# One step of a hybrid diffusion backbone on one core: running sums started in PSUM by ScalarE, units turned, products and head squares moved to ScalarE

## The chip, the core and the metric

The kernel runs on one core of one Trainium2 chip. The metric is the device time of one execution in microseconds (us), as the median of several runs. Five engines work side by side, each through its own list of instructions in order: PE (TensorE, the matrix multiplier), DVE (VectorE), ACT (ScalarE), POOL (GpSimd) and SP (SyncE, which here only issues DMAs). PE writes its sums to PSUM, which this kernel uses as 8 banks of 128x512 fp32; everything else lies in SBUF.

## The reference

Two groups of 128 tokens (a context group, `s=0`, and a latent group, `s=1`), width 2048, go through one layer.

```python
sh1, sc1, g1, sh2, sc2, g2 = split(silu(c) @ w_ada + b_ada, 6)
h = rms_norm(x, norm1_w) * (1 + sc1) + sh1                 # 128 x 2048 each group
qa, ka, va, qb, kb, vb, ga, gb = split(h @ w_in)           # 2048 -> 8704 columns
oa, ob = attention(qa, ka, va), attention(qb, kb, vb)      # QK-norm, rotary, softmax
merged = sigmoid(ga) * (oa @ w_br_a) + sigmoid(gb) * (ob @ w_br_b)
x = x + g1 * (merged @ w_out)
h2 = rms_norm(x, norm2_w) * (1 + sc2) + sh2
x = x + g2 * (relu(h2 @ w_up) ** 2 @ w_down)               # 2048 -> 8192 -> 2048
```

All inputs and outputs are fp32.

## The kernel before

**A step.** The weights are read once, in tiles of 128x1024 (512 KB: two blocks of 128 rows by 512 columns). A step of the kernel is the work on one such tile; there are 456, in an order fixed when the kernel is built. To reach fp32 accuracy each tile is split: ACT copies it to the type fp32r (`wH`, L93), DVE takes the difference tile minus copy (`wL`, L241), and PE forms three products for each pair of operands: high by high, high by low, low by high (L291 to L293 in a `unit`, L391 to L393 in the first stage). An ordinary step has 12 matmuls of 128x512 (2 row blocks x 2 token groups x 3 products). The two token groups have a PSUM bank each.

**What sets the order.** Every engine's list is written out by hand in `run` (L264): for each step it first issues the DMA loads that the table `RUN` makes due, then splits tiles up to `LOOK` steps ahead, then writes the step's matmuls and, at a unit's end, its evacuation, and last what is hung on that step with `at`. So an instruction of ACT or DVE waits behind all that was written before it, above all behind the splits of later tiles. The pool `pacc` has 4 banks, given out in turn; the pool `paux` has the other 4.

**First stage, the K passes.** The projection `h @ w_in` for nine column blocks (units qA 0 and 1, kvA, qB 0 and 1, kB 0 and 1, vB 0 and 1) goes over the 16 row blocks of K in five passes (`CHUNKS`: 2, 2, 2, 4, 6 row blocks), because `h` becomes known bit by bit: PE, in `pair_mm`, computes the modulation (sc1, sh1) from `w_pair` between the steps. In each pass every unit starts two fresh banks; at its end the sum is copied to SBUF by ACT in the first pass (`first_evac`, L372), and added to the SBUF sum by DVE in the later four (L400). A unit of the passes of 2 row blocks is one step. Passes 1 and 2 are steps 9 to 17 and 18 to 26.

**Middle.** The eight gate units, and between their steps the attention: `qk_stat` (L618) squares the heads on ACT and sums the squares on DVE (L624); `normalise` (L740) multiplies the softmax numerators by 1/denominator on DVE (L746). Then the branch products, `w_out`, the second norm (`norm2`, L970) and the first two units of `w_up`.

**Last stage, up pairs and down pieces.** The 8192 columns of `w_up` are done as 8 pieces of two blocks. Seven of them are "pairs" (`up_pair`, L1107) in which some row blocks, listed in `FAST`, use Strassen's scheme: 7 products in place of 8. For such a fast position DVE forms sums of weight blocks (`prep_y`, L1164: `t` L1172, then L1175 to L1177, then the low parts `XL`, `tL`, `uL`, L1180 to L1182) and ACT the high parts (`XH`, `YB`, `tH`, `uH`). A pair uses all 8 banks: Q1, Q6, Q2, Q7 of `pacc`, Q3, Q4, Q5, Z of `paux`. After each pair come four down units (`down_unit`, L1246), one for each block of 512 output columns, over that piece's 1024 rows of `w_down`: 4 steps each. A down unit's two banks are copied to `dsum` by ACT for piece 0, added to `dsum` by DVE (L1257), or, where listed in `SUM_DMA`, copied by ACT and added by a DMA that POOL issues. `gate_sum` (L1234) multiplies `dsum` by g2 and adds it to x at piece 6; the last piece multiplies its own banks by g2 and adds (`resid`, L902).

**The places that matter below.** A pair begins while the last down unit's banks are being emptied: its second product takes the bank of that unit's first group, its third the bank of the second group. A pair ends with five products (Q2, Q7, Q4, Q5, Q3) after Q6; the down unit behind it takes the banks of Q1 (first group) and Q6 (second group). `silu_cond` (L1307) computes SiLU of the condition row each time it is loaded (`load_cond`, L1302), five times two rows in all.

Of the kernel before, what the change touches and what calls it, by code (L numbers as in the profile page):

```python
# [18 lines left out]
P = 128  # L19
# [15 lines left out]
H_AT = 41  # L35
DOTS1 = [11, 17, 20, 28, 28, 31, 34, 37]
# [5 lines left out]
GATE_BACK = 8  # L42
DIRECT = (3,)
LO_DMA = [70, 83, 107, 131, 176, 184, 233, 292, 314, 328, 402, 404]
LO_AHEAD = 2

LOOK = "443323444122344433223333332123333453344534333554455544344534333543324554444555556665556644444333333333332222122312344544555434333333342344333334333323445566643344456656533344434444445455564546555553444554322355444554433333333434334533333333333654544332334455543444555653215536544523333334543233333332223323365455455443222212233432443334434642333334444544534434333333333325434222223333434444444434555642255353443444442222432331122132223342112223332233345544"
RUN = "301110000000010212223333322222222221111122244455544355434445554334554445555664543433234334444445665543321222222212444444444444442222222232223344444455544544444444555455454445566644455555554543365434343355445756644443566664333312222234552332223333334545332333333333322211122222332233322212233323323332332112344444442343322211333343334323233334544422742222212223445554422333233322222211222333333435767545333110221112232111233456655566567556433435335553333334"
CONST_AT = [65, 67]
XL_DMA = []  # L50
ADA_AT = [None, 4, 13, 18, 21, 36, 29]
XS_AT = {1: 13, 2: 18, 3: 29}
POST = {('kvA', 0): [67, 70, 75], ('qA', 0): [70, 73, 78], ('qA', 1): [72, 74, 80], ('kB', 0): [77, 83, 90], ('qB', 0): [82, 84, 93], ('kB', 1): [86, 91, 93], ('qB', 1): [90, 93, 97]}
JOBS = [[79, 80, 80, 87, 93], [81, 83, 88, 90, 93], [87, 87, 89, 90, 99], [93, 93, 96, 99, 102], [96, 97, 100, 105, 112], [102, 103, 107, 112, 123], [105, 107, 111, 118, 123], [112, 115, 118, 121, 123]]
SS_AT = [43, 51, 73, 75, 139, 139]
T_AT = [4, 4]
PREP_IN = [6, 7]
DOTS = [33, 39, 42, 43, 47, 47, 48, 49, 52, 54, 55, 57, 60, 62, 69, 70, 73, 77, 80, 84, 90, 91, 92, 92, 94, 98, 101, 103, 103, 105, 108, 110, 111, 112, 115, 118, 120, 121, 122, 122, 126, 127, 128, 129, 130, 132, 132, 136, 137, 138, 138, 143, 144, 147, 147, 150, 153, 155, 157, 161, 164, 167, 170, 172, 173, 174, 175, 176, 177, 178, 179, 182]
DOTS2 = [230, 232, 234, 235, 236, 237, 240, 243, 255, 263, 265, 269, 270, 288, 301, 301, 307, 328, 328, 331, 333, 334, 358, 360, 361, 363, 366, 368, 391, 391, 395, 399]
STAT_AT = [-1, 0, 10, 16]  # L60
T_PAIR = [[8, 9], [6, 8], [8, 9], [7, 8], [10, 11], [8, 9], [12, 11]]
P_PAIR = [[4, 2], [2, 4], [3, 4], [1, 3], [6, 6], [3, 3], [6, 5]]
M_TE = (3,)
M_AT = [1, 3, 9]
FLIP = 1
P_UP = [4, 1]
# [5 lines left out]
def tile_hybrid_step(ctx: ExitStack, tc: tile.TileContext, a):  # L72
# [210 lines left out]
    def mm3(acc, stat, st, first, last, order=(0, 1)):  # L283

        wh, wl = st["hl"]
        for k in range(2):
            kk = 2 * st["half"] + k
            for tb in order:
                sh, sl = stat(kk, tb)
                f, l = first and k == 0, last and k == 1  # L290
                pe.matmul(acc[tb], sh, wh[:, k, :], start=f, stop=False)  # L291
                pe.matmul(acc[tb], sh, wl[:, k, :], start=False, stop=False)  # L292
                pe.matmul(acc[tb], sl, wh[:, k, :], start=False, stop=l)  # L293
# [77 lines left out]

    def first_evac(u, acc):  # L372
        units[u] = G(f"u_{u[0]}{u[1]}").rearrange("p (s n) -> p s n", s=2)
        for tb in range(2):
            copy(units[u][:, tb, :], acc[tb])

    def start_steps(u, k0, nk):

        box = {}

        def mm(st, kt):
            if kt == 0:
                box["acc"] = [bank("acc", pacc) for _ in range(2)]
            acc = box["acc"]
            wh, wl = st["hl"]
            last = kt + 2 == nk
            for k in range(2):
                g, kg = divmod(k0 + kt + k, 4)
                for tb in range(2):
                    sh, sl = hH[g][:, kg, tb, :], hL[g][:, kg, tb, :]  # L390
                    pe.matmul(acc[tb], sh, wh[:, k, :], start=kt == 0 and k == 0, stop=False)  # L391
                    pe.matmul(acc[tb], sh, wl[:, k, :], start=False, stop=False)  # L392
                    pe.matmul(acc[tb], sl, wh[:, k, :], start=False, stop=last and k == 1)  # L393
            if not last:
                return
            if k0 == 0:
                first_evac(u, acc)
                return
            for tb in range(2):
                dve.tensor_tensor(units[u][:, tb, :], units[u][:, tb, :], acc[tb], op=OP.add)  # L400
            box.clear()

        for kt in range(0, nk, 2):
            add_step(wsrc(w_in, k0 + kt, COL[u[0]] + 512 * u[1]), lambda st, kt=kt: mm(st, kt), u)
# [18 lines left out]
    for g, i in XS_AT.items():  # L423
        at(i, lambda g=g: x_scale(g))
    k0 = 0
# [1072 lines left out]
```

## Time and profile before

| | |
|---|---|
| runs, median (lowest to highest) of 3 | 1333.61 us (1331.23 to 1334.71) |
| profiled execution, first to last instruction | 1331.3 us |
| PE busy | 1316.0 us (99%), 6411 instructions recorded |
| DVE busy | 1190.2 us (89%), 1546 |
| ACT busy | 800.8 us (60%), 979 |
| POOL busy | 54.6 us (4%), 64 |
| DMA | 392 MB, mean 295 GB/s |

The profiled execution is one more execution than the three runs; its own time is given as its span, 1331.3 us from the first to the last instruction. That is 2.3 us under the median of the runs and equal to the fastest of them.

In the lists by line, a row gives line, engine, operation, written tile, read tiles, shapes and count, then the busy time in us and the mean of one in ns, then the engine's idle time just before and what ended it. In the windows, each engine has its busy time and, in brackets, its count. In the timeline a row gives start and duration in us; a matmul's duration is 0.39 us because matmuls overlap, so for PE the distance between starts is what counts.

### The profile page before, as it was taken

The numbers are of one execution on the slowest core, as the hardware profiler recorded it, in microseconds if no ns is written. First come the engines' busy times: TensorE is split into PE (matmuls) and PEld (weight loads), VectorE is DVE, ScalarE is ACT, GpSimd is POOL, SyncE is SP. The second block draws the span as 40 slices with busy tenths as digits, with TensorE's granted clock in tenths as the row PEclk, the third lists the DMA queues.
The fourth block names the chain that finished last, engine by engine and source line by source line (L and its number), as shares of the span: only waits on it lengthen the run. The fifth ranks groups of instructions, "written<-read, shape, count | busy, mean of one in ns | idle before, by whom it ended". The sixth has DMA issues, their size and how long they took to land.

```text
span 1331.3 us, 18039 instructions
## 1 busy us (share of the span) xinstructions
PE 1316.0 (99%) x6411; PEld 1067.0 (80%) x6412; DVE 1190.2 (89%) x1546; ACT 800.8 (60%) x979; POOL 54.6 (4%) x64
## 2 busy tenths in 40 slices
PE   8999999999999999999999999999999999999998
PEld 4777778788888878888888888888888888877887
DVE  4699999988898999999779998998999999989685
ACT  5534443476656446635677866758577576676660
POOL 0000000521000000000000000000000000000000
PEclk9999999999999999999999999999999999999999
DMA  9999998986589999996578876988798696878962
GB/s 374 409 409 408 409 401 300 384 277 240 177 329 355 381 392 356 354 367 214 191 230 280 281 254 215 291 273 266 235 296 255 237 301 206 311 195 291 331 213 98
DMA packets 148267, 392.24 MB, mean 295 GB/s; under 512 B 51793, under 2 KB 53009, under 8 KB 148177
## 3 DMA queue, kind: packets, MB, share of 16 engines
q1 hardware_dynamic: 144448, 378.16, 78.8%
q0 software_dynamic: 3584, 12.85, 5.0%
q8 instruction: 50, 0.82, 0.3%
q14 instruction: 41, 0.33, 0.1%
q10 hardware_dynamic: 144, 0.08, 0.0%
HBM read 367.16 MB, written 8.68 MB: 282 GB/s over the span
## 4 chain that ended last, share of the span: by engine, by line
PE 92%; DMA 4%; DVE 2%; ACT 1%; issue 1%; SPq 0%; DVEq 0%; ACTq 0%
PE acc L291 16%; PE acc L292 16%; PE acc L293 16%; PE Q L1117 6%; PE Q L1119 6%; PE Q L1118 6%; PE acc L391 4%; PE acc L392 4%; PE acc L393 4%; DMA araw<-in_w_pair 3%; PE ps_ada L308 2%; PE ps_S L707 1%; PE Z L1119 1%; PE Z L1117 1%; PE Z L1118 1%; DMA aT<-in_w_adaT 1%
## 5 line engine op out<-in xcount | busy, mean ns | idle before, releaser
L241 DVE TENSOR_TENSOR wL<-raw,wH 128x1024 fp32r<-128x1024 f32 x375 | 446.6, 1225 | 72.0 <-ACT wH L93 67.9
L93 ACT ACTIVATE wH<-raw 128x1024 fp32r<-128x1024 f32 (+1 forms) x393 | 392.8, 1044 | 128.3 <-PE acc L392 23.3
L391 PE MATMUL acc<-wH,hH 128*128 128x512 f32 x276 | 109.1, 395 | 0.0
L393 PE MATMUL acc<-wH,hL 128*128 128x512 f32 x276 | 107.5, 390 | 0.0
L392 PE MATMUL acc<-wL,hH 128*128 128x512 f32 x276 | 107.5, 389 | 0.0
L291 PE MATMUL acc<-wH,hH 128*128 128x512 f32 x256 | 101.4, 396 | 0.0
L293 PE MATMUL acc<-wH,hL 128*128 128x512 f32 x256 | 99.7, 390 | 0.0
L292 PE MATMUL acc<-wL,hH 128*128 128x512 f32 x256 | 99.7, 390 | 0.0
L1327 DVE CUSTOM_DVE_ANT_0 aT<-aT,cB,cols 128x1024 f32<-128x1024 f32 x56 | 71.7, 1286 | 0.2
L1327 DVE CUSTOM_DVE_ANT_0 junk<-aT,cB,cols 128x1024 bf16<-128x1024 f32 x56 | 71.4, 1280 | 0.0
L93 ACT ACTIVATE tH<-t 128x1024 fp32r<-128x1024 f32 x33 | 35.0, 1061 | 58.0 <-DVE t L1172 55.4
L391 PEld LDWEIGHTS acc<-wH,hH 128*128 128x128 f32 x276 | 51.8, 188 | 13.6 <-issue 2.5
L393 PEld LDWEIGHTS acc<-wH,hL 128*128 128x128 f32 x276 | 51.8, 188 | 11.0
L392 PEld LDWEIGHTS acc<-wL,hH 128*128 128x128 f32 x276 | 51.8, 188 | 10.4
L293 PEld LDWEIGHTS acc<-wH,hL 128*128 128x128 f32 x256 | 48.0, 188 | 10.2
L291 PEld LDWEIGHTS acc<-wH,hH 128*128 128x128 f32 x256 | 48.1, 188 | 9.8 <-ACT sq L622 0.4
L292 PEld LDWEIGHTS acc<-wL,hH 128*128 128x128 f32 x256 | 48.1, 188 | 9.4
L93 ACT ACTIVATE uH<-raw 128x1024 fp32r<-128x1024 f32 x33 | 35.1, 1063 | 31.6 <-DVE raw L1177 28.6
L1223 ACT ACTIVATE up<-up 128x1024 f32<-128x1024 f32 x28 | 29.7, 1062 | 26.8 <-DVE up L1217 26.3
L308 PE MATMUL ps_ada<-araw,cpad 128*32 128x256 f32 x640 | 39.1, 382 | 2.7 <-DMA araw<-in_w_pair 2.5
L93 ACT ACTIVATE fTa<-pTa 128x2048 uint16<-128x2048 uint16 x16 | 40.5, 2533 | 2.0 <-PE acc L292 1.4
L1172 DVE TENSOR_TENSOR t<-raw 128x1024 f32<-128x1024 f32 x33 | 40.2, 1219 | 1.0 <-PE acc L292 1.0
(641 smaller groups left out, 3316.7 us busy)
## 6 DMA issues: line engine op xcount, KB each, us to landing
raw<-in_w_in SPq DMA_DIRECT2D x133, 512.0 KB, 9.5
raw<-in_w_down SPq DMA_DIRECT2D x128, 512.0 KB, 5.6
araw<-in_w_pair SPq DMA_DIRECT2D x80, 512.0 KB, 10.2
raw<-in_w_upF SPq DMA_DIRECT2D x66, 512.0 KB, 5.2
aT<-in_w_gT SPq DMA_DIRECT2D x64, 512.0 KB, 6.9
raw<-in_w_up SPq DMA_DIRECT2D x62, 512.0 KB, 5.0
aT<-in_w_adaT SPq DMA_DIRECT2D x48, 512.0 KB, 9.6
raw<-in_w_out SPq DMA_DIRECT2D x32, 512.0 KB, 9.6
```

The costliest lines, as they stand in the source:

```text
L93: act.activation(out, in_, AF.Copy)
L241: dve.tensor_tensor(st["lo"], st["raw"], st["hi"].bitcast(F32), op=OP.subtract)
L291: pe.matmul(acc[tb], sh, wh[:, k, :], start=f, stop=False)
L292: pe.matmul(acc[tb], sh, wl[:, k, :], start=False, stop=False)
L293: pe.matmul(acc[tb], sl, wh[:, k, :], start=False, stop=l)
L391: pe.matmul(acc[tb], sh, wh[:, k, :], start=kt == 0 and k == 0, stop=False)
L392: pe.matmul(acc[tb], sh, wl[:, k, :], start=False, stop=False)
L393: pe.matmul(acc[tb], sl, wh[:, k, :], start=False, stop=last and k == 1)
L1117: pe.matmul(acc, stat[0], hi, start=f, stop=False)
L1118: pe.matmul(acc, stat[0], lo, start=False, stop=False)
L1119: pe.matmul(acc, stat[1], hi, start=False, stop=l)
L1327: dve.tensor_tensor_reduce(out, box["raw"], cB[s, tag], 1.0, dst if second else baT[:, part, fb:fb + 1], OP.mult, OP.add, dst)
```

## The change

PE has the same 6020 instructions before and after (counted in the two built programs, with the same operands and shapes). What changes:

- **Down pieces.** A down unit of piece 1 to 7 no longer starts fresh banks. Ahead of it ACT copies the SBUF sum `dsum` into its two banks (`seed`, 56 copies), and its matmuls add on top. At its end ACT copies the banks back to `dsum` (56 copies in place of 28), except in the last piece. The 28 DVE additions, the 10 additions by DMA and `gate_sum` (16 DVE operations) go. The seed is written after the third step before the unit; for the first down unit behind a pair it stands at the end of that pair.
- **K passes.** Of the later passes' units, 22 are seeded in the same way (44 copies in, 44 copies out in place of 44 of the DVE additions). Two more units per pass boundary stay in their banks: passes 1 and 3 run the units in a turned order that begins with vB, so the last two units of one pass are the first two of the next, and 16 further additions go. 12 of 72 remain.
- **Attention.** The product with 1/denominator is 32 ACT instructions of 128 or 256 columns in place of 8 on DVE; the squares are 52 ACT instructions of 128 columns with a running sum in place of 14 wider ones and 7 DVE reductions.
- **Strassen.** In `prep_y` the DVE's order is now t, YB, first sum, XL, second sum, tL, uL. `FAST` keeps its counts (3, 4, 5, 5, 5, 5, 6) and moves positions.
- **Rest.** SiLU of the condition is computed 4 times in place of 10, kept in DRAM and loaded again. `resid` multiplies both groups before it adds. x and g2 are loaded back 8 steps before a unit's end in piece 7, where it was 6 in piece 6. Tables are set anew: `LOOK` at 59 of 456 places and `RUN` at 98, and the places of dot products, attention parts and loads.

ScalarE's list around the start of pair 7, before. `dsum_10517` and `dsum_10694` are the copies that empty the third and fourth down unit's banks; XH, YB, tH, uH are one fast position.

```order
L93 ACTIVATE a13H<-fTa_10566 128x1024
L93 ACTIVATE wH<-raw 128x1024 x2
L93 ACTIVATE XH<-raw 128x1024
L93 ACTIVATE YB<-raw 128x512
L93 ACTIVATE tH<-t_10614 128x1024
L93 ACTIVATE uH<-raw 128x1024
L93 ACTIVATE XH<-raw 128x1024
L93 ACTIVATE YB<-raw 128x512
L93 ACTIVATE tH<-t_10659 128x1024
L93 ACTIVATE uH<-raw 128x1024
L93 ACTIVATE dsum_10694<-acc 128x512 x2
L93 ACTIVATE XH<-raw 128x1024
```

The same place of ScalarE's list in the changed kernel, from the third unit's seed on (`dsum_7148` is the sum of the third unit, `dsum_7219` of the fourth).

```order
L97 ACTIVATE XH<-raw 128x1024
L97 ACTIVATE dsum_7148<-acc 128x512 x2
L97 ACTIVATE YB<-raw 128x512
L97 ACTIVATE tH<-t_10699 128x1024
L97 ACTIVATE uH<-raw 128x1024
L97 ACTIVATE wH<-raw 128x1024 x2
L97 ACTIVATE dsum_7219<-acc 128x512 x2
L97 ACTIVATE XH<-raw 128x1024
L97 ACTIVATE YB<-raw 128x512
L97 ACTIVATE tH<-t_10780 128x1024
L97 ACTIVATE uH<-raw 128x1024
```

The fourth unit's copies moved from behind two fast positions to behind one, with two plain splits between them and it.

ScalarE's list in pass 1 of the changed kernel, from the end of step 10 on (`acc<-u_...` is a seed, `u_...<-acc` the emptying of a unit's banks). Before, this stretch holds splits, modulation work and no copy of a sum.

```order
L97 ACTIVATE u_vB_615<-acc 128x512 x2
L97 ACTIVATE acc<-u_qB_391 128x512 x2
L97 ACTIVATE u_kvA_348<-acc 128x512 x2
L97 ACTIVATE acc<-u_qB_408 128x512 x2
L97 ACTIVATE wH<-raw 128x1024 x2
L97 ACTIVATE u_qB_391<-acc 128x512 x2
L97 ACTIVATE acc<-u_kB_470 128x512 x2
L97 ACTIVATE wH<-raw 128x1024 x2
L97 ACTIVATE u_qB_408<-acc 128x512 x2
L97 ACTIVATE S<-ps_ada 128x512
L97 ACTIVATE acc<-u_kB_511 128x512 x2
```

Each unit's seed stands two units ahead of its matmuls, behind the emptying of the unit whose banks it takes.

ScalarE's list at the end of pair 2 in the changed kernel: `up<-Q` reads bank Q1, and the row behind it seeds the banks of Q1 and Q6 for the first down unit.

```order
L97 ACTIVATE wH<-raw 128x1024 x3
L97 ACTIVATE up_7527<-Q_7231 128x512
L97 ACTIVATE acc<-dsum_6938 128x512 x2
L1267 ACTIVATE up_7527<-up_7527 128x1024 x2
L1267 ACTIVATE up_7528<-up_7528 128x1024 x2
```

The seed was not there before; relu and square (two rows each) now stand behind it.

The core of the diff:

```diff
-FAST = {1: (0, 3, 7), 2: (0, 2, 6, 7), 3: (0, 2, 4, 5, 7), 4: (0, 2, 4, 5, 7), 5: (0, 3, 4, 5, 7), 6: (0, 2, 4, 5, 7), 7: (0, 1, 2, 4, 5, 7)}
-SUM_DMA = [5, 6, 11, 13, 16, 19, 21, 23, 25, 27]
+FAST = {1: (0, 4, 7), 2: (0, 4, 6, 7), 3: (0, 2, 3, 4, 7), 4: (0, 2, 4, 5, 7), 5: (0, 1, 3, 5, 7), 6: (0, 2, 4, 5, 7), 7: (0, 2, 3, 4, 5, 7)}
+SEED_AT = 3
+KEEP = True
+SEED1_AT = 2
+SEED1 = "111111111111111100100001101011111111"
...
+        def seed():
+            seeds1[u] = banks()
+            for tb in range(2):
+                copy(seeds1[u][tb], units[u][:, tb, :])
...
-            if kt == 0:
-                box["acc"] = [bank("acc", pacc) for _ in range(2)]
+            if kt == 0 and u not in held:
+                if seeded and u not in seeds1:
+                    seed()
+                held[u] = seeds1.pop(u) if seeded else banks()
+                opened[u] = not seeded
...
-                    pe.matmul(acc[tb], sh, wh[:, k, :], start=kt == 0 and k == 0, stop=False)
+                    pe.matmul(acc[tb], sh, wh[:, k, :], start=opened[u] and k == 0, stop=False, skip_group_check=skip)
...
+    turned = first_units[7:] + first_units[2:7] + first_units[:2]
...
         for s in range(2):
-            act.activation(sq[:, s].rearrange("p h d -> p (h d)"), raw[:, s, 0:nh * HD], AF.Square)
-        ssq, r = SM(2 * nh, "ssq"), SM(2 * nh, "rq")
-        dve.tensor_reduce(ssq.rearrange("p (s h) -> p s h", s=2), sq, axis=AX.X, op=OP.add)
+            for h in range(nh):
+                act.activation(sq[:, s, h, :], raw[:, s, h * HD:h * HD + HD], AF.Square,
+                               accum_out=ssq[:, s * nh + h:s * nh + h + 1])
...
-            dve.tensor_tensor(prob[:, :, 0:nk], prob[:, :, 0:nk], rd.unsqueeze(2).to_broadcast([P, 4, nk]), op=OP.mult)
+            for h in range(4):
+                act.activation(prob[:, h, 0:nk], prob[:, h, 0:nk], AF.Copy, scale=rd[:, h:h + 1])
...
-                dve.tensor_tensor(Y[:, 0:512], t[:, 0:512], X[:, 512:1024], op=OP.add)
                 dve.tensor_tensor(b["YB"][:, 512:1024], Y[:, 512:1024], b["YB"][:, 0:512].bitcast(F32), op=OP.subtract)
+                dve.tensor_tensor(Y[:, 0:512], t[:, 0:512], X[:, 512:1024], op=OP.add)
+                if 8 * p + pos not in XL_DMA:
+                    dve.tensor_tensor(b["XL"], X, b["XH"].bitcast(F32), op=OP.subtract)
                 dve.tensor_tensor(Y[:, 512:1024], Y[:, 0:512], Y[:, 512:1024], op=OP.add)
                 copy(b["uH"], Y)
...
+                    if p > 1:
+                        seed(p - 1, 0)
...
+    def seed(p, n):
+
+        seeds[p, n] = [bank("acc", pacc) for _ in range(2)]
         for s in range(2):
-            dve.tensor_tensor(d[:, s, :], d[:, s, :], gbc["g2", n][:, s, :], op=OP.mult)
-            dve.tensor_tensor(x1[n][:, s, :], x1[n][:, s, :], d[:, s, :], op=OP.add)
+            copy(seeds[p, n][s], dsum[n][:, s, :])
...
+        if p and (n or p == last):
+            at(len(wsteps) - SEED_AT, lambda: seed(p, n))
```

More of the change, by code (lines that the diff above doesn't have):

```diff
@@ L65 @@
 FLIP = 1
-P_UP = [4, 1]
+P_UP = [2, 1]
 T_UP = [6, 5]
@@ L281, in run, with mm3 @@
                 fn()
-    def mm3(acc, stat, st, first, last, order=(0, 1)):
+    def mm3(acc, stat, st, first, last, seeded=False):
         wh, wl = st["hl"]
@@ L1067, in mm @@
                 if q == 0:
-                    box["acc"] = [bank("acc", pacc) for _ in range(2)]
+                    box["acc"] = seeded()
                 box["hl"][q] = st["hl"]
@@ L1269, in down_unit @@
-        if p == last - 1:
-            at(end_of(("down", p, n)) + 6, lambda: gate_sum(n))
+        unit(a["w_down"], 512 * n, [4 * j for j in PIECES[p]], stat, evac, ("down", p, n), seeded if p else None)
     for n in PIECES[0]:
```

184 lines of the change are left out of this document (106 added, 78 removed).

## The prediction, made before the changed kernel was run

> **What bounds the kernel now.** I read the page first, then the same busy times stage by stage, then the list of what PE waited for, and last the timeline around the one wait that is large.
>
> ```profile
> span 1331.3 us, 18039 instructions
> ## 1 busy us (share of the span) xinstructions
> PE 1316.0 (99%) x6411; PEld 1067.0 (80%) x6412; DVE 1190.2 (89%) x1546; ACT 800.8 (60%) x979; POOL 54.6 (4%) x64
> ```
>
> PE is busy for 99% of the span. The change leaves PE's 6020 instructions as they are, so the 94 us or so that it takes from DVE, and the 131 us that it gives ACT (the counts of the change by the durations below), are worth nothing by themselves. Only what PE waits for can go or come. The stages show where that is (us; busy time and count of PE, weight loads, DVE, ACT, POOL; granted clock, DMA share, GB/s). The rows are the stages of pairs 1, 3, 4 and 7, then passes 1 and 2, then the attention.
>
> ```profile
> 730.46:773.98 43.52, 43.52 (x194) 36.04 (x192) 41.75 (x53) 34.63 (x36) 0.00 (x0) 1.00 0.83 276
> 858.30:898.82 40.52, 40.41 (x178) 33.14 (x177) 40.00 (x45) 22.27 (x25) 0.86 (x1) 1.00 0.85 281
> 942.34:983.16 40.82, 40.42 (x179) 33.15 (x177) 38.84 (x42) 24.70 (x28) 1.73 (x2) 1.00 0.84 288
> 1194.45:1239.26 44.81, 41.21 (x175) 33.67 (x174) 43.75 (x48) 25.03 (x29) 0.87 (x1) 0.96 0.90 309
> 53.10:81.88 28.78, 28.78 (x177) 22.56 (x176) 27.39 (x40) 12.40 (x16) 0.00 (x0) 1.00 1.03 408
> 81.88:114.98 33.10, 33.10 (x246) 24.86 (x244) 30.67 (x51) 14.84 (x19) 0.00 (x0) 1.00 1.03 409
> 233.00:466.00 233.00, 233.00 (x1189) 193.00 (x1188) 210.88 (x298) 136.34 (x243) 33.52 (x31) 1.00 0.84 306
> ```
>
> The first row is PE unhindered: 43.52 us / 192 matmuls = 226.7 ns from one start to the next. At that rate the 177 matmuls of pairs 3 and 4 take 40.13 us, and took 0.39 and 0.69 more. The 174 of pair 7 take 39.45 us, and took 44.81: **5.4 us too many**, with a granted clock of 0.96. PE's own waits, in us in total, times, longest:
>
> ```profile
> PE Q L1117 <- ACT dsum L93: 4.0, 2, 3.6
> PE ps_ada L308 <- DMA araw<-in_w_pair: 2.5, 5, 0.6
> PE acc L461 <- ACT hH L93: 1.3, 2, 0.9
> ```
>
> All else is below 1.3 us. The first row is pair 7's wait. PE's timeline there, the releaser in brackets:
>
> ```profile
> 1195.58 0.39 PE L1119 MATMUL Q<-YB,h20L 128*128 128x512 f32 x1
> 1199.57 0.80 PE L1117 MATMUL Q<-tH,sH 128*128 128x512 f32 x1 [3.60 <-ACT dsum L93]
> 1200.16 0.63 PE L1118 MATMUL Q<-tL,sH 128*128 128x512 f32 x1
> ...
> 1202.72 0.43 PE L1118 MATMUL Q<-tL,sH 128*128 128x512 f32 x1
> ```
>
> Start to start, 1195.58 to 1199.57 is 3.99 us, 3.76 more than 0.227. Then the matmuls start 0.43 us apart until 1202.72: half the rate, another 1.6 us. ACT's rows in that time:
>
> ```profile
> 1197.97 1.06 ACT L93 ACTIVATE uH<-raw 128x1024 fp32r<-128x1024 f32 x1 [1.00 <-DVE raw L1177]
> 1198.94 1.06 ACT L93 ACTIVATE dsum<-acc 128x512 f32<-128x512 f32 x2
> ```
>
> 1195.58 is the pair's sixth matmul, so the down unit's last one started 6 x 0.227 before, at 1194.22, and its banks could have been emptied from about 1194.5. The two copies stand in ACT's list behind the highs of two fast positions, and the last of these, `uH`, waited for DVE. The copies began 4.4 us late.
>
> **The change, part by part.** The sums go against the profiled span, 1331.3 us; the median of the runs is 2.3 us above it, and I add that at the end.
>
> *Pair 7.* In the new list the two copies stand behind one fast position and two plain splits, and that position's ACT work stands behind the third unit's copies, which can run four steps (48 x 0.2267 = 10.9 us) before the pair. So ACT is free in time, and 5.4 us are there to win. What is late next is DVE:
>
> ```profile
> 1201.20 1.22 DVE L1172 TENSOR_TENSOR t<-raw 128x1024 f32<-128x1024 f32 x1
> ...
> 1207.80 2.35 DVE L241 TENSOR_TENSOR wL<-raw,wH 128x1024 fp32r<-128x1024 f32 x2
> ...
> 1231.00 1.22 DVE L1182 TENSOR_TENSOR uL<-raw,uH 128x1024 fp32r<-128x1024 f32 x1
> ```
> ```profile
> 1235.41 0.39 PE L1118 MATMUL Q<-uL,sH 128*128 128x512 f32 x1
> ```
>
> A fast position takes DVE 6.60 us (1201.20 to 1207.80) and PE 21 x 0.2267 = 4.76. A plain one takes DVE about 2.3 and PE 5.44. So DVE loses 1.8 us per fast position and lives on its lead. Before, the last `uL` was ready at 1232.2 and used at 1235.4: 3.2 us of lead, less than the 5.4 that PE is to gain. The new order (0, 2, 3, 4, 5, 7) puts a plain position second. Counted from the pair's start: ACT empties the banks until 1.2, does XH (1.0) and YB (0.6) of position 2 by 2.7; DVE can do `YB` then and, five operations later, has that position's `uL` at about 8.0. Three more fast positions, the plain one and the last (4 x 6.5 + 2.3; 6.5 since the new order no longer makes an operation wait for the one just ahead of it) end at 36.3, or at 35.9 if each takes 6.4. PE wants that `uL` after 34.7 + 4 x 0.2267 = 35.6. I take 0.3 us of wait there (0 to 2.2, the latter if DVE stands to PE as before). Three splits (3.4 us) and the additions stand behind it on DVE, so the seed after the pair is late too, another 0.2. **Pair 7: -4.9 us (-5.4 to -3.2).**
>
> *Pairs 3 and 4.* There, too, ACT now empties the last unit's banks behind a single high part, `XH`. That needs a load to have landed, so I take most of the excess as gone, not all: **-0.3** (-0.4 to 0) and **-0.4** (-0.7 to 0). Pair 5's second position is now fast; by the same count DVE has its `uL` at 7.1 where PE wants it at 8.4.
>
> *Passes 1 and 2.* Durations, as busy us and mean ns:
>
> ```profile
> L93 ACT ACTIVATE dsum<-acc 128x512 f32<-128x512 f32 x28 | 16.0, 594 | 24.3 <-PE acc L293 22.5 <-PE acc L292 1.2
> L93 ACT ACTIVATE wH<-raw 128x512 fp32r<-128x512 f32 x6 | 3.5, 619 | 0.0
> L980 ACT ACTIVATE h2f<-x,r 128x512 f32<-128x512 f32 x4 | 2.7, 713 | 0.5 <-POOL r L136 0.5
> L1257 DVE TENSOR_TENSOR dsum<-dsum,acc 128x512 f32<-128x512 f32 x28 | 18.2, 683 | 2.7 <-PE acc L293 2.7
> ```
>
> Between the ends of steps 9 and 24, 15 ordinary steps with some modulation matmuls between them (53.7 us of PE), ACT gets 28 copies out (0.594) and 24 copies in. A copy from SBUF to PSUM does not occur in the trace. Nearest is the SBUF to SBUF copy of the same shape at 0.619; the ends are 0.594 (the PSUM read) and 0.713. I take 0.619, the row with the same source. That adds 16.6 + 14.9 = 31.5 us to what ACT did there: 12.40 + 14.84 us in 61.9, so 23.6 in 53.7. Together 55 us, less some 3 to 6 since two copies in a row overlap (1.06 us in place of 1.19): 50 us of 53.7. ACT becomes nearly full where it was 44% busy. It keeps up on the whole, and each seed stands two units (5.4 us) ahead. I take **+0.5 us**. The lower end is 0, since PE waits for no bank there now; the upper is 2.9: 0.5 more, and 24 x 0.1 should each seed cost 0.1 more than assumed with nothing to hide it. DVE, 27.39 of 28.78 us busy there, loses 18 units x 2 x 0.683 = 24.6 us, and nothing waited for it.
>
> *Ends of pairs 2 to 7.* The first down unit needs its second bank, Q6's, seeded after DVE's second addition.
>
> ```profile
> 813.46 2.80 DVE L1217 TENSOR_TENSOR up<-up,Q 128x512 f32<-128x512 f32 x4
> ```
> ```profile
> 814.78 0.39 PE L291 MATMUL acc<-wH,a2H 128*128 128x512 f32 x1
> ```
> ```profile
> 1066.78 1.40 DVE L1217 TENSOR_TENSOR up<-up,Q 128x512 f32<-128x512 f32 x2
> ```
> ```profile
> 1067.65 0.40 PE L291 MATMUL acc<-wH,a8H 128*128 128x512 f32 x1
> ```
>
> After pair 2 the addition ends at 814.14 and a copy of 0.62 at 814.8; the bank is wanted three matmuls after 814.78, at 815.46: 0.6 us to spare. After pair 5 the addition ends at 1067.46, the copy at 1068.1, the bank is wanted at 1067.65: **+0.5 us** (0 to 1.0, if one of the others slips). The seeds of the other down units stand three steps (about 8 us) ahead of need.
>
> *Attention.*
>
> ```profile
> L732 ACT ACTIVATE prob<-ps_S,nm 128x128 f32<-128x128 f32 x16 | 5.7, 367 | 10.5 <-DVE nm L730 7.7 <-DVE nm L728 2.7
> ...
> L732 ACT ACTIVATION_READ_ACCUMULATOR prob<-ps_S,nm 128x1 f32 x24 | 4.9, 203 | 0.0
> ...
> L622 ACT ACTIVATE sq<-u_qB 128x512 f32<-128x512 f32 x4 | 2.3, 634 | 0.0
> ```
>
> The squares: 52 x (0.367 + 0.203) less 14 x 0.634 is +20.8 us of ACT. The 32 scalings are 12 to 20 us (0.367 to 0.62 each). In the attention's 233 us ACT would then be busy for some 175 in place of 136.34, and PE never waits there: **0** (0 to 1, where a weight split stands behind such a group). [...]
>
> *The rest.* SiLU, `resid` and the loads change nothing that PE waits for: loads keep their place in SP's list apart from a few steps, and POOL loses ten transfers. The early waits for `araw` and `hH` (3.8 us) keep their causes: **0** (0 to -3.8).
>
> The sum: -4.9 - 0.3 - 0.4 + 0.5 + 0.5 = **-4.6**, a span of 1326.7. With the median's 2.3 us: **1329.0 us**.
>
> **Rivals.** A measurement of this kernel tells 0.3%, 4.0 us, from no change: faster is below 1329.6, slower above 1337.6.
>
> *DVE takes over pair 7, or the wait stays in part.* If DVE stands to PE as it does now, PE gains only DVE's lead: the 5.4 us shrink to 3.2, the sum to -2.9 or, with the other terms at their poor ends, to about 0: 1330.7 to 1334. For it speaks DVE's 43.75 us of work in a stage of 39.45; against it the plain second position and two additions fewer ahead of the pair. On the clock, 1199.57 to 1202.72 shows that the long wait cost 1.6 us beyond itself, and no other row shows how long a wait must be for that. [...]
>
> *Slower: ACT as the gate of all banks.* Every unit now needs ACT twice, and ACT's list is in order. If ACT comes to a down unit's banks as late as it did at pair 7 (5.4 us) at two of the seven pair starts, the sum is -4.6 + 10.8: 1339.8. One such place gives 1334.4, still no change; two decide it. For it: at pairs 3 to 5 the copies stand behind an `XH` that waits for a load. Against it: the same arrangement at pair 4 cost 0.7.
>
> *More than the forecast.* The waits for `araw` and `hH` shrink too, since DVE has room early: up to 3.8 us more, 1325.2.
>
> **How the numbers follow.** The forecast has 0.54 (0.46 of it below 1329.6, 0.08 in the band), the first rival 0.23, all in the band, the slower one 0.13 (0.11 slower, 0.02 in the band), the last 0.10. That makes faster 0.56, same 0.33, slower 0.11. The range: the forecast's own terms give 1326.5 to 1333; it reaches down to 1322.5 for the last rival with the good ends, and up to 1336 for one late bank and DVE's wait together; beyond lie some 0.15 to 0.2.
>
> **What would show it.** In the new profile pair 7's stage should be near 39.9 us with a clock of 1.00, without a wait for `dsum` above 1 us, and with a small wait for `uL` or the second seed at its end; pairs 3 and 4 near 40.2; ACT nine tenths busy or more in passes 1 and 2, PE's rate there unchanged; a wait of about 0.5 us for `acc` after pair 5. It is wrong if PE waits for ACT's seeds in passes 1 and 2 by over 3 us in all, or for DVE by over 2 us in pair 7, or for `dsum` at several pair starts.

## The result, and the profile after

The changed kernel takes **1336.01 us** (median of 10 runs, 1333.60 to 1338.58) against 1333.53 for the kernel before: a ratio of **1.0021** (95% interval 1.0013 to 1.0029). It is a little slower, where 1329.0 and faster was forecast; it lies just past the upper end, 1336.0, of the range that was given. A ratio here is not the quotient of the two medians beside it and can lie to either side of that. A run's time is 1.7 to 2.2 us longer than its span from the first to the last instruction (here 1335.19 against 1333.4), so the span before, 1331.3, belongs to an execution near the median of its runs and not to the fastest.

The page of the changed kernel (to be read beside the first rows of the prediction; the profiled run itself took 1335.19 us):

```profile
span 1333.4 us, 18150 instructions
## 1 busy us (share of the span) xinstructions
PE 1316.8 (99%) x6412; PEld 1065.2 (80%) x6412; DVE 1105.9 (83%) x1421; ACT 899.1 (67%) x1267; POOL 47.7 (4%) x58
```

DVE has lost 84 us and ACT has gained 98 (94 and 131 were forecast), and PE's busy time has hardly moved. What moved are PE's waits (total, times, longest):

```profile
PE ps_ada L312 <- DMA araw<-in_w_pair: 2.8, 6, 0.6
PE acc L295 <- ACT acc L97: 2.2, 1, 2.2
PE Q L1159 <- DMA wL<-in_w_up: 1.6, 1, 1.6
...
PE Q L1158 <- ACT dsum L97: 0.6, 2, 0.4
...
PE acc L296 <- DVE wL L245: 0.5, 1, 0.5
PE ps_gr L1393 <- DVE gc_g L1380: 0.4, 1, 0.4
...
PE Q L1159 <- DVE uL L1223: 0.2, 1, 0.2
```

The wait of 3.6 us for `dsum` is gone. The other six rows shown are waits that the kernel before did not have or had smaller. By stage (us, then busy time and count of PE, weight loads, DVE, ACT, POOL; clock, DMA share, GB/s): pairs 2, 3 and 7, then passes 1 and 2.

```profile
775.29:816.81 41.52, 41.10 (x182) 33.72 (x180) 39.07 (x44) 24.30 (x28) 0.00 (x0) 1.00 0.72 261
862.79:904.83 42.04, 40.48 (x178) 33.08 (x177) 38.74 (x44) 24.65 (x29) 0.87 (x1) 1.00 0.75 257
1200.47:1240.43 39.96, 39.74 (x176) 32.58 (x174) 39.52 (x42) 24.39 (x30) 0.00 (x0) 1.00 0.84 309
53.10:81.88 28.78, 28.78 (x178) 22.50 (x177) 18.51 (x25) 25.34 (x42) 1.23 (x2) 1.00 1.03 408
81.88:114.98 33.10, 33.10 (x246) 24.86 (x245) 20.60 (x33) 26.67 (x44) 0.49 (x1) 1.00 1.03 409
```

Pair 7 takes 39.96 us where it took 44.81, at full clock. Pair 3 takes 42.04 where it took 40.52, and pair 2 41.52 where it took 40.80. Passes 1 and 2 take PE the same time as before, with ACT 25.34 of 28.78 us busy instead of 12.40, and 26.67 of 33.10 instead of 14.84.

Since PE's work is the same, the two profiles can be laid side by side by PE's own milestones (the starts and ends of the pairs). Each number is how much longer the stage took than in the profile before, in us; the stages that aren't named differ by less than 0.01. The kernels below are the experiments of the next section.

```
stage                   after   e5    e10    e11    e6    e12
up to pair 1            +1.31 +1.86  +1.23  +1.20 +1.30  +0.18
pair 2                  +0.72 +0.48  +0.31  +0.05  0.00  +0.03
downs behind pair 2     +2.46  0.00   0.00  +1.14  0.00   0.00
pair 3                  +1.52 +3.95  +0.05  -0.37 +0.28  +0.17
downs behind pair 3      0.00  0.00  +0.18  +2.05  0.00   0.00
pair 4                  -0.22 -0.69  -0.69  +0.94 -0.33  -0.35
downs behind pair 4      0.00  0.00   0.00  +0.54  0.00   0.00
pair 5                  -0.17 -0.17  -0.17  -0.05 -0.15  -0.15
downs behind pair 5     -0.04 -0.04  +0.06  +0.47 -0.03  -0.03
pair 6                   0.00 +1.27  +1.93  +0.49  0.00   0.00
downs behind pair 6     +0.44 -0.13  -0.11  +5.28 +0.01  +0.01
pair 7                  -4.85 -3.51  -3.60  -4.79 -3.63  -4.77
behind pair 7           +0.92 +0.89  +0.89  +0.96 +0.85  +0.84
sum                     +2.08 +3.90  +0.09  +7.92 -1.71  -4.08
```

The first row moves by up to 2 us from one execution to the next: e6 and e12 have the first part of before unchanged and show +1.30 and +0.18, and e3, which has it too, +2.02. In the changed kernel's profile the row has another origin. There PE is 0.12 us earlier than before when the K passes are nearly done (at 212 us), and loses 0.53 us between there and 450 us, the stretch with the attention, 0.77 between 472 and 492 us, and 0.13 near 650.

**Where the largest new wait comes from.** PE at the start of the fourth down unit behind pair 2, and ACT's list ahead of it, in the changed kernel:

```profile
849.22 0.39 PE L297 MATMUL acc<-wH,a3L 128*128 128x512 f32 x1
851.77 0.50 PE L295 MATMUL acc<-wH,a2H 128*128 128x512 f32 x1 [2.17 <-ACT acc L97]
```
```profile
844.76 1.06 ACT L97 ACTIVATE wH<-raw 128x1024 fp32r<-128x1024 f32 x1 [1.56 <-DMA raw<-in_w_down]
845.73 2.52 ACT L97 ACTIVATE fTa<-pTa 128x2048 uint16<-128x2048 uint16 x1
848.28 1.06 ACT L97 ACTIVATE a5H<-fTa 128x1024 fp32r<-128x1024 f32 x1
849.25 1.99 ACT L97 ACTIVATE wH<-raw 128x1024 fp32r<-128x1024 f32 x2
851.14 1.10 ACT L97 ACTIVATE acc<-dsum 128x512 f32<-128x512 f32 x2
```

The first row is the split for the very step that PE waits to begin. It waited for its load, 3.6 us of a transposed tile came next, then the splits of the two steps after, and only then the seed. Its low part was ready at 847.1 (DVE) and its banks had been emptied at 840.1, which leaves the seed.

### The profile page after: what moved, and what is told of

It reads as the page before. It is cut to its first block, busy times and chain, and to the rows that moved or that the text cites. A ratio compares the mean times of both kernels' runs of the same rounds, so it can differ in the third digit from the quotient of the medians.

```text
span 1333.4 us, 18150 instructions
## 1 busy us (share of the span) xinstructions
PE 1316.8 (99%) x6412; PEld 1065.2 (80%) x6412; DVE 1105.9 (83%) x1421; ACT 899.1 (67%) x1267; POOL 47.7 (4%) x58
## 4 chain that ended last, share of the span: by engine, by line
PE 82%; DMA 10%; ACT 3%; DVE 2%; issue 1%; SPq 0%; ACTq 0%; DVEq 0%
PE acc L295 15%; PE acc L296 15%; PE acc L297 15%; DMA araw<-in_w_pair 6%; PE Q L1159 6%; PE Q L1158 6%; PE Q L1160 6%; PE acc L412 4%; PE acc L414 3%; PE acc L413 3%; DMA raw<-in_w_in 1%; ACT wH L97 1%; PE ps_ada L312 1%; PE ps_S L744 1%; DMA cB<-in_crow 1%
## 5 line engine op out<-in xcount | busy, mean ns | idle before, releaser
L97 ACT ACTIVATE acc<-dsum 128x512 f32<-128x512 f32 x56 | 31.7, 590 | 15.3 <-DVE t L944 7.7
L1223 DVE TENSOR_TENSOR uL<-raw,uH 128x1024 fp32r<-128x1024 f32 x33 | 40.4, 1225 | 1.5
```

Of the source, the lines that this page charges most:

```text
L97: act.activation(out, in_, AF.Copy)
```

## The experiments

The kernel before, measured alongside each, has a median of 1332.7 to 1333.4 us.

**e1: seeds one step earlier.**
```diff
-SEED_AT = 3
+SEED_AT = 4
```


> The changed kernel with every down unit's seed written one step earlier (four steps before the unit in place of three). Theory: in the changed kernel the seed of the fourth down unit behind pair 2 stands in ScalarE's list behind two plain splits, a transposed tile's copy and its high part, comes 2.2 us late, and PE's 2.33 us wait there is its price. One step earlier it stands ahead of the tile's copy; the wait goes and nothing else moves: about 1333.7 us against 1336.0 of the changed kernel, that is level with the kernel before (1333.5), and the wait for acc by ScalarE is gone from PE's list. Rival: the weights come late there anyway (the splits waited for their loads), so PE waits for the next split instead: 1335.5 or more.

Measured: 1335.71 us, ratio 1.0021 (1.0013 to 1.0030). The wait behind pair 2 is gone and no time with it. ACT's rows at pair 3's start in this kernel, and PE's:

```profile
858.39 1.06 ACT L97 ACTIVATE uH<-raw 128x1024 fp32r<-128x1024 f32 x1 [1.88 <-DVE raw L1220]
859.36 1.07 ACT L97 ACTIVATE dsum<-acc 128x512 f32<-128x512 f32 x2
860.31 2.00 ACT L97 ACTIVATE wH<-raw 128x1024 fp32r<-128x1024 f32 x2
862.21 1.06 ACT L97 ACTIVATE XH<-raw 128x1024 fp32r<-128x1024 f32 x1
863.15 1.08 ACT L97 ACTIVATE dsum<-acc 128x512 f32<-128x512 f32 x2
```
```profile
863.80 0.50 PE L1158 MATMUL Q<-tH,sH 128*128 128x512 f32 x1 [1.70 <-ACT dsum L97]
```

The third unit's banks were full at about 849.6 and were emptied at 859.4, the fourth's at 863.2. The wait went from the seed to the emptying: ACT's list was late as a whole, not at one place. My theory, a single late seed, falls; its rival was nearer, though it was the copies and not the weights that came late.

**e2 and e2b: the low part by DMA in pair 3.** e2 takes step 292 out of `LO_DMA`; e2b puts pair 3's positions back.
```diff
-LO_DMA = [70, 85, 107, 119, 130, 176, 184, 233, 292, 314, 393, 404]
+LO_DMA = [70, 85, 107, 119, 130, 176, 184, 233, 314, 393, 404]
```
```diff
-3: (0, 2, 3, 4, 7)
+3: (0, 2, 4, 5, 7)
```


> The changed kernel with one low part less by DMA: that of the second step of pair 3's position 6 is formed by VectorE, as most are. Theory: that transfer starts late because ScalarE's copy that feeds it stands behind three fast positions in a row, on which VectorE falls behind; PE's 1.72 us wait for it goes, VectorE has 1.2 us more to do and a lead to pay it from: about 1334.2 us. Rival: VectorE is as late as the transfer was, and PE waits for its split or for the last uL of pair 3: 1336, no gain.

> The changed kernel with pair 3's fast positions as before, (0, 2, 4, 5, 7) in place of (0, 2, 3, 4, 7). Theory: with a plain position between the fast ones VectorE is not behind when the low part by DMA is due, the transfer starts earlier and PE's 1.72 us wait goes: about 1334.2 us. Rival: the wait belongs to the place of that transfer in the lists and stays, 1336; or another wait comes at the pair's end.

In the changed kernel ACT's rows, POOL's issue of the transfer, the same issue in the kernel before, and PE's wait for it in the changed kernel read:

```profile
881.21 1.06 ACT L97 ACTIVATE uH<-raw 128x1024 fp32r<-128x1024 f32 x1 [1.86 <-DVE raw L1220]
882.17 1.04 ACT L97 ACTIVATE wH<-raw 128x1024 fp32r<-128x1024 f32 x1
883.25 1.06 ACT L251 ACTIVATE wL<-wH 128x1024 fp32r<-128x1024 f32 x1
```
```profile
884.61 0.87 POOL L252 DMA_DIRECT2D wL<-in_w_up  x1 [166.32 <-DMA raw<-in_w_upF]
```
```profile
876.50 0.86 POOL L248 DMA_DIRECT2D wL<-in_w_up  x1 [19.67 <-ACT wL L247]
```
```profile
894.71 0.50 PE L1159 MATMUL Q<-wL,h23H 128*128 128x512 f32 x1 [1.56 <-DMA wL<-in_w_up]
```

ACT's copy stands behind the `uH` of the third fast position in a row, which waits for DVE. The transfer starts at 884.6 and PE wants its result at 893.0; before, it started at 876.5. In both experiments pair 3's stage falls from +1.52 to -0.37 and -0.41: this part of both theories is shown. The medians do not show it: e2 1337.93 (ratio 1.0036, 1.0017 to 1.0055, runs from 1332.6 to 1345.1), e2b 1334.99 (1.0023, 1.0009 to 1.0038, up to 1344.9). What one long run loses can be seen in e2's profiled run, 1343.5 us. ACT, around 1190:

```profile
1191.65 2.48 ACT L97 ACTIVATE fTa<-pTa 128x2048 uint16<-128x2048 uint16 x1 [8.77 <-DMA pTa<-pla]
1194.16 1.06 ACT L97 ACTIVATE a13H<-fTa 128x1024 fp32r<-128x1024 f32 x1
1195.13 1.10 ACT L97 ACTIVATE acc<-dsum 128x512 f32<-128x512 f32 x2
```

The transposing transfer `pTa<-pla` took up to 17.0 us to land in this run (median 4.3). ACT waited 8.77 us for it with the seed behind, and PE waited 7.7 us for the seed. Before, no seed stood behind that copy. The long runs of e2b, e8 and e9 have no profile; but runs above 1340 us come only in kernels with the seeded pieces (e2, e2b, e7, e8, e9 and e11, and e13 to e15, which are slower throughout), and none of e3, e5, e6, e10 and e12, which lack these, or of the kernel before is above 1337.7.

**e3 and e6: pair 7 alone, on the kernel before.** e3 turns pair 7's positions; e6 adds the changed order of DVE's sums in `prep_y`.
```diff
-7: (0, 1, 2, 4, 5, 7)}
+7: (0, 2, 3, 4, 5, 7)}
```


> The kernel before with one edit: pair 7's fast positions (0, 2, 3, 4, 5, 7) in place of (0, 1, 2, 4, 5, 7), its sums still emptied by VectorE, POOL and ScalarE as before. Theory: the order of positions alone takes the two copies from behind the second fast position, and gives VectorE its lead: pair 7's 5.4 us shrink to 1 or less, about 1329 us. Rival: the seeds, the lookahead or the new order of VectorE's sums were needed for it: 1332 to 1333.5.

> The kernel before with two edits: pair 7's fast positions (0, 2, 3, 4, 5, 7) and the changed order of VectorE's sums in prep_y (YB before the first sum, XL before the second). Theory: with the positions alone (1330.45 us) PE's 1.7 us wait in pair 7 was for XL of position 5, which the new order has ready about 0.7 us earlier and whose chain it shortens by 0.1 us per position: 1.7 shrinks to about 0.7, 1329.5 us. Rival: VectorE is simply the bound there and PE waits for uL in its place: 1330.5, no change.

Measured: e3 1330.45 us (0.9982, 0.9973 to 0.9991), e6 1330.43 (0.9982, 0.9973 to 0.9991). The turn alone takes the wait for `dsum` away, without a seed; in its place PE waits for DVE. In e3's list of waits:

```profile
PE Q L1118 <- DVE XL L1180: 1.5, 1, 1.5
```

With DVE's new order (e6) this falls to 0.4 us, and one of 0.6 for `uL` stands at the pair's last position: DVE is the bound there, as e6's rival said, and the order of sums alone changes the total by nothing that can be measured.

**e12: more lead for DVE.** e6 with one more down unit ahead of pair 7 summed by POOL's transfer.
```diff
-SUM_DMA = [5, 6, 11, 13, 16, 19, 21, 23, 25, 27]
+SUM_DMA = [5, 6, 11, 13, 16, 19, 21, 22, 23, 25, 27]
```


> The kernel before with pair 7's positions, VectorE's order in prep_y, and one more down unit (the third behind pair 6) summed by POOL's transfer in place of VectorE. Theory: VectorE is what bounds pair 7 now (waits for XL, uL and the first split behind it, 2.0 us in all), and 1.2 us less ahead of the pair take about 0.8 of it: 1329.6 us. Rival: VectorE's lead is set by when ScalarE forms the highs, or ScalarE's two copies come too late: 1330.4 or more.

Measured: **1329.65 us**, ratio 0.9978 (0.9969 to 0.9987), the lowest median of all kernels here, though its interval overlaps those of e3 and e6. In its list:

```profile
PE Q L1118 <- DVE uL L1182: 0.3, 1, 0.3
```

Pair 7's stage is 4.77 us shorter than before, 1.14 shorter than in e6: the additions that DVE did ahead of the pair were what was left.

**e5, e10, e11: the seeded pieces, taken out and put in.** e5 is the changed kernel with the down pieces as before; e10 is e5 with the fast positions of pairs 1 to 6 as before, too. e11 goes the other way: e6 with the seeded pieces, and the tables of before. The core of the part, as e11 puts it in and e5 and e10 take it out:
```diff
+        if p and (n or p == last):
+            at(len(wsteps) - SEED_AT, lambda: seed(p, n))
...
             for s in range(2):
-                    dve.tensor_tensor(dsum[n][:, s, :], dsum[n][:, s, :], acc[s], op=OP.add)
+                copy(dsum[n][:, s, :], acc[s])
```


> The changed kernel with the down pieces as before: fresh banks, sums added by VectorE or by POOL's transfers, gate_sum at piece 6, g2 and x loaded back then; everything else of the change stays. Theory: what the change loses it loses at the piece's seeds and copies, which stand in ScalarE's one list behind transposed tiles and splits that wait for transfers: the 2.33 us wait behind pair 2, the 0.6 at pair 2's start and the scattered long runs go, pair 7 keeps most of its gain (about 1 us of it goes to VectorE's additions), and the wait for the low part in pair 3 (1.7) stays: about 1332.5 us, with runs no wider than those of before. Rival: the loss sits in the attention, the K passes or the tables; then it stays at 1335 or more.

> The changed kernel with the down pieces as before and the fast positions as before in pairs 1 to 6, so that of the last stage only pair 7's positions, VectorE's order in prep_y and the tables remain. Theory: the pieces' seeds and the moved positions of pairs 3 and 5 are what the change loses; without them there stay some 1.3 us up to pair 1 and pair 7's gain of about 2.6: about 1331.5 us. Rival: the tables or the early parts cost more than that: 1333.5 or more.

> The kernel before with pair 7's positions, VectorE's order in prep_y (these two: 1330.43 us) and the down pieces in seeded banks as in the change, with the tables of before. Theory: the seeds put ScalarE's list in PE's way at the down units; VectorE's freed time is worth 1 us at pair 7, the seeds cost 2 to 5 us, and more in single runs: 1332 to 1335 us with a wide spread, and PE's list of waits names ScalarE's copies into acc. Rival: the seeds are harmless and only the changed tables made them late: 1329.5 us.

e11: 1339.57 us, ratio 1.0049 (1.0036 to 1.0062), 9 us above e6. PE's list of waits there:

```profile
PE acc L292 <- ACT acc L94: 3.9, 4, 1.8
...
PE Q L1119 <- ACT dsum L94: 1.8, 3, 1.2
```

So the seeds cost 9 us under the old tables, at almost every down section (see its column): the theory holds, its size of 2 to 5 us was too small. e5 is the other half: the +2.46 behind pair 2 goes to 0.00, and behind pair 6 there stands -0.13. But e5 as a whole, 1336.64 us (1.0024, 1.0016 to 1.0033), is no faster than the changed kernel, and my 1332.5 missed. Its column says why: the wait for the low part in pair 3 was worse in the profiled run (+3.95, half-rate matmuls among it), pair 7 gained 1.3 less, and at pair 6's start PE waited for `dsum`: where POOL's transfer sums a unit, ACT still empties its banks, and the changed tables had put a transposed tile just ahead of that. e10 has that wait again (+1.93), and 1334.58 us (1.0011, 1.0003 to 1.0020) where I expected 1331.5. The tables and the pieces hang together; taking one out leaves the other's price, and no run here takes both out and keeps the rest.

**e7: the tiles behind the seeds.**
```diff
-T_PAIR = [[10, 9], [6, 8], [6, 9], [7, 10], [10, 14], [8, 9], [12, 14]]
+T_PAIR = [[10, 9], [6, 10], [6, 10], [7, 10], [10, 14], [8, 10], [12, 14]]
```


> The changed kernel with the transposed tiles of pieces 4, 5, 7 and 13 copied one to two steps later, so that each stands behind the fourth unit's seed in ScalarE's list and not just ahead of it. Theory: the tile's copy waits for a transposing transfer whose landing varies (4 to 17 us), and the seed behind it makes PE wait; with the order turned the long scattered runs (up to 1338.6) go and the wait behind pair 2 shrinks: median 1334.5 us, highest below 1336.5. Rival: ScalarE's list is late as a whole there, and as with the seed written a step earlier the wait reappears at pair 3's start: median 1335.5 or more.

Measured: 1337.74 us, ratio 1.0031 (1.0020 to 1.0043). PE has no wait for a seed left in the profile, and waits 2.1 us for `dsum` at pair 3's start and 1.6 at pair 7's. As in e1, the rival holds.

**e8 and e9: attention back on DVE; no seeds in the K passes.** Both are the changed kernel with one part undone; e8 puts back the attention's lines of before, and e9's edit is this:
```diff
-SEED1 = "111111111111111100100001101011111111"
+SEED1 = "000000000000000000000000000000000000"
```


> The changed kernel with the head squares in wide ScalarE instructions plus VectorE sums, and the softmax product on VectorE, both as before. Theory: the 52 narrow instructions and 32 scalings cost PE only two short waits at 315 to 322 us (0.9 us together): 1335.3 us, within the noise of the changed kernel. Rival: VectorE, which takes back some 17 us, makes PE wait elsewhere in the attention: 1336.5.

> The changed kernel without the 22 seeds of the K passes: those units start fresh banks and VectorE adds them, as before; the turned order and the units that stay in their banks remain. Theory: ScalarE keeps up with the seeds in the passes and PE waits for none there, so nothing changes: 1336 us, within 0.7. Rival: the seeds do cost in the passes: 1335 or less.

e8: 1335.39 us (1.0025, 1.0011 to 1.0040); PE loses 0.19 us between 212 and 450 us, the stretch with the attention, where the changed kernel loses 0.53, so that part costs about 0.3 us. e9: 1335.52 (1.0036, 1.0016 to 1.0056). Passes 1 and 2 take the same time with and without seeds. Neither part decides anything.

**e13 to e15: the pieces' seeds on DVE.** e13 puts all 56 on DVE; e14 adds e7's tiles and e2b's positions; e15 has only the second to fourth unit's seeds of pieces 1 to 6 on DVE, with e2b's positions.
```diff
-            copy(seeds[p, n][s], dsum[n][:, s, :])
+            dve.tensor_copy(seeds[p, n][s], dsum[n][:, s, :])
```


> The changed kernel with the 56 seeds of the down pieces copied by VectorE in place of ScalarE, at the same places of the program. Theory (ScalarE's list is the cause): the waits for acc behind pairs 2 and 6 shrink by what ScalarE's list adds; but VectorE's list has the tile's low part ahead of the seed, which waits for ScalarE's high part, so half of the wait stays: about 1334.5 us. Rival (seeding as such): the same waits, now named VectorE: 1336 us or more.

> As e13, with the tiles' copies of pieces 4, 5, 7 and 13 behind the fourth unit's seed, and pair 3's fast positions as before. Theory: the seed then waits neither for a tile nor in ScalarE's list, and the low part by DMA is in time; what is left over the kernel before is some 1.3 us of the early parts, against pair 7's 3.9: about 1331 us. Rival: seeding as such costs: PE still waits for acc at two or more down units, 1334 us or more.

> The changed kernel with pair 3's fast positions as before, and with the seeds of the second to fourth down unit of pieces 1 to 6 copied by VectorE (the first unit's and piece 7's stay on ScalarE). Theory: VectorE has some 17 percent of idle time in the down units and stands nearer to PE than ScalarE, so the waits for acc behind pairs 2 and 6 halve and ScalarE's copies at the pair starts come earlier: 1333.5 us. Rival (any in-order list will do): VectorE's list waits for ScalarE's highs and for the tiles as well, and the waits keep their size or grow: 1335 us or more, as with pair 3's old positions alone (1335.0).

All three missed: 1370.15 us (1.0282, 1.0268 to 1.0296), 1370.41 (1.0278, 1.0264 to 1.0292) and 1347.08 (1.0110, 1.0092 to 1.0128). e13's list, and DVE's rows at the end of its pair 2:

```profile
PE acc L295 <- DVE acc L1290: 26.3, 7, 5.3
```
```profile
814.42 2.87 DVE L1258 TENSOR_TENSOR up<-up,Q 128x512 f32<-128x512 f32 x4
817.21 1.28 DVE L1258 TENSOR_TENSOR up<-Q,up 128x512 f32<-128x512 f32 x2
818.52 0.69 DVE L1258 TENSOR_TENSOR up<-up,Z 128x512 f32<-128x512 f32 x1
819.12 0.68 DVE L1258 TENSOR_TENSOR up<-up,Q 128x512 f32<-128x512 f32 x1
819.72 1.28 DVE L1290 COPY acc<-dsum 128x512 f32<-128x512 f32 x2
```

The seed of the first unit stood behind the pair's additions, so e13 and e14 could not tell what they were made for; e15 leaves those seeds on ACT. There DVE's seeds behind pair 2 and pair 3 are late too (6.72 and 3.94 us more than before in those stages): they stand behind splits that wait for ACT's highs. (Behind pair 6, 5.33 us more, PE waits for ACT; that was not taken apart.) So it is not ScalarE as an engine: in both lists tried, a seed is late by what the list has ahead of it.

## Why the prediction was wrong, point by point

**Pair 7: right.** The stage was to be 39.9 us at full clock and is 39.96; the small wait for `uL` was to be 0.3 and is 0.22 in the list, 0.38 counted from start to start. The stage is 4.85 us shorter, and 4.9 was forecast for it and a small loss behind it. (The forecast's terms, 39.45 and 0.3, make 39.75; 39.9 has the 0.2 behind the pair in it.) e3, e6 and e12 show the reason that was given: the plain second position frees the copies, and DVE is what is late next. The loss behind the pair was taken as 0.2 us and is larger. PE's next wait and ACT's rows before it:

```profile
1249.53 0.50 PE L296 MATMUL acc<-wL,a13H 128*128 128x512 f32 x1 [0.46 <-DVE wL L245]
```
```profile
1245.12 2.15 ACT L1267 ACTIVATE up<-up 128x1024 f32<-128x1024 f32 x2 [0.37 <-DVE up L1258]
1247.18 1.04 ACT L97 ACTIVATE wH<-raw 128x1024 fp32r<-128x1024 f32 x1
```

DVE's late additions hold ACT's relu and square, and these hold the next split. The six kernels of the table and e3, all with the new positions, lose there (+0.84 to +0.96), so the net gain is 3.9 us, not 4.9.

**The seeds between down units: this step failed.** The prediction gave them one sentence: they "stand three steps (about 8 us) ahead of need", and a price of nothing. The seed is written after the third step before the unit, so 2 x 12 x 0.2267 = 5.4 us ahead, not 8; and in ACT's list it stands behind all splits that were written by then, up to six steps ahead of PE, and behind the transposed tiles. The cost is 2.46 us behind pair 2 in this execution; behind pair 6 none (the 0.44 there are a wait for a row of g2 that DVE sums), but 10.8 us in e2's. With the tables of before, the seeded pieces cost 9 us (e11 against e6). In the changed kernel `LOOK` has ACT 4 to 6 steps ahead when a seed is written behind pairs 2 and 6, and 1 to 4 behind the other pairs; no run lowered it there. The underlying count is one of slack. Before, a unit's banks had to be emptied until the unit after next began, one unit or 10.9 us later, by an addition on DVE or a copy on ACT. Now they must be emptied and filled again in the same 10.9 us, both by ACT. e1 and e7 show the exchange: what the seed is given, the emptying lacks.

**Pair 3: -0.3 forecast, +1.52 measured.** I checked DVE's lead for pair 5's moved positions and not what pair 3's do to ACT's list: three fast positions in a row held the copy that feeds a low part by DMA. e2 and e2b show it: without that wait the stage is 0.37 and 0.41 us shorter than before, as was forecast.

**Pair 2: 0 forecast, +0.72 measured.** The fourth down unit's copies stand behind two splits there and are 0.6 us late. The prediction spoke of the starts of pairs 3 to 5 only.

**Pair 4** -0.4 forecast, -0.22 measured; **passes 1 and 2** +0.5 forecast, nothing measured, with or without the seeds (e9); ACT was busy for 45.81 of the 53.78 us from the end of step 9 to that of step 24, where 50 was forecast; a copy into PSUM takes 0.59 us for `dsum`, where I took 0.619. **Ends of pairs** +0.5 forecast: no wait of PE for the first unit's seed is in the list. **Attention** 0 forecast, about 0.3 (e8). The 0.77 us between 472 and 492 us stand where the changed kernel runs 64 modulation matmuls in two groups, with other products between them and a wait of 0.19 for `araw`, and the kernel before in one; no run tests it.

**The sum.** In the profile the change was to be -4.6 us and is +2.08. Of the 6.7 us between them 2.5 are the seeds, 1.8 pair 3, 1.3 the part up to pair 1, 1.0 the loss behind pair 7, 0.7 pair 2, 0.4 the row of g2 and 0.2 pair 4; two losses of 0.5 that did not come, and 0.2 us at pair 5, go the other way. In the prediction's working three readings are off without weight: the first row of its table of stages is not pair 1 but the four down units behind it (192 matmuls, so the rate of 226.7 ns stands), Q6's bank is free after DVE's first addition (the time used is that one's), and the terms' ends add up to 1327.1 and 1335.3 us, not to 1326.5 and 1333.

**Of the rivals,** the slower one had the mechanism, ACT's list ahead of PE's banks, and the wrong place: it looked for it at the starts of pairs, with pair 7's price. The larger part of it came at the seeds, in smaller pieces, and pair 7's gain covered most of the sum. How long a wait must be to cost the clock, which no row of before showed, stays open: two runs lost the rate after a wait of 1.8 us, and one kept it (below).

## What to carry to other kernels

Before an addition is replaced by a bank that starts from the old sum, count what the bank has to go through between two uses and who does it: emptying late cost nothing here until the bank was needed again (e1's third unit behind pair 2: 9.8 us from full to the first copy, and no wait of PE up to the end of the fourth unit), filling late stopped PE at once (2.17 us behind pair 2). Behind splits for later steps, or behind a copy that waits for a transfer of uneven landing, such a copy is as late as they are (ACT's 8.77 us for the tile in e2 became 7.7 us of PE's). It would belong into a list that does not work ahead, which no run here tried. An engine's idle share says nothing about this: ACT was busy for 67% of the span, and the price did not fall when DVE, with its freed time, did the copies (1347.08 to 1370.41 us in e13 to e15).

## What the runs showed of the hardware that was not expected

**Half rate after a short wait.** In the kernel before, a wait of 3.6 us was followed by matmuls at half rate (granted clock 0.50 from 1199.57 to 1202.72), which cost 1.6 us. In e5 a wait of 1.8 us was followed by it as well:

```profile
893.36 0.50 PE L1160 MATMUL Q<-wL,h23H 128*128 128x512 f32 x1 [1.80 <-DMA wL<-in_w_up]
893.70 0.39 PE L1161 MATMUL Q<-wH,h23L 128*128 128x512 f32 x1
893.93 0.50 PE L1159 MATMUL Q<-wH,h23H 128*128 128x512 f32 x1
894.23 0.63 PE L1160 MATMUL Q<-wL,h23H 128*128 128x512 f32 x1
```

From 894.23 on the starts are 0.43 us apart, seven times, and from 897.58 on 0.23 again; some 1.5 us are lost. It begins 0.9 us after PE has resumed. e11 shows the same after 1.78 us. But e9 has a wait of the same length as e5 at the same step and keeps its rate (the mean granted clock of that execution is 1.000, of e5's 0.998):

```profile
893.23 0.50 PE L1159 MATMUL Q<-wL,h23H 128*128 128x512 f32 x1 [1.80 <-DMA wL<-in_w_up]
893.56 0.40 PE L1160 MATMUL Q<-wH,h23L 128*128 128x512 f32 x1
```

In the changed kernel a wait of 2.17 us (at 851.77) left the rate alone, too (granted clock 1.00 from 851.77 to 855). The length of a wait alone did not decide it here; what else did, no run shows.

**A transposing transfer's landing varies.** `pTa<-pla` took 4.2 to 17.0 us in e2, 4.2 to 10.7 in the kernel before, the same 16 transfers each time. Before, where only work far ahead of PE depended on it, ACT waited for it once, for 0.5 us, and PE's list of waits has no row that goes back to it.
